# Ordering a mixture of experts by token count: blocks of two and of four experts, and the place of the overflow loop

## The chip, the cores and the metric

The kernel runs on one core of one Trainium2 chip. The metric is the device time of one execution in microseconds, 1274.82 us before the change (median of 3 runs, 1274.45 to 1277.62).

## The reference

An encoder trunk of two layers over 256 tokens of width 1024, in float32. Each layer is a mixer (layer 0: differential and latent attention; layer 1: dilated attention), a residual with layer norm, a hierarchical mixture of experts (MoE), and a second residual with layer norm. The MoE is what the change touches:

```
coarse = x @ w_group + b_group;  g = argmax(coarse)              # one of 4 groups
fine   = (x @ w_route + b_route)[group g]                        # 8 experts in it
top_v, top_i = top_k(fine, 2)                                    # 2 experts per token
gate   = softmax(coarse)[g] * softmax(top_v)
y     += gate * (silu(x @ w_gate[e]) * (x @ w_up[e])) @ w_down[e]   # for each chosen e
```

There are 32 experts; each has 1024 x 512 values in w_gate and in w_up and 512 x 1024 in w_down, 6 MiB in all. A layer has 512 assignments of a token to an expert, so an expert gets 16 on the average. Which expert gets how many is known only when the router has run.

## The kernel before, in words

**Stages.** The program is traced in one pass: mixer of layer 0, its MoE, mixer of layer 1, its MoE. Nearly all weights come through one ring of 16 tiles of 1 MiB (`RING`, `piece`, line 69), each filled by one DMA that SP issues. SP issues in order and waits until the tile's former content has been used. A planner orders the instructions of each engine when the program is built; `tc.issue_after` adds orders by hand.

**Routing** (`mixer_norm`, `halves`, `route`). TensorE makes the router's logits. On DVE, `route` finds for each token its group and its two experts, and with a matmul against a triangle the token's rank within each expert (`key`). `weights_of` makes the gates. `crowded` counts, for each expert, how many times 64 slots are overfull; the sum is the number of rounds of the overflow loop, `n_i`. All this stands at the start of a MoE, ahead of and beside the first gather.

**Pairs of experts.** The experts are taken in their own order, two at a time, 16 pairs a layer, with 64 token slots each (`CAP`). For every two pairs, `select` (L474) makes a one-hot matrix of 4 x 64 slots from `key`, and `gather` (L499) multiplies it with the normed tokens, in a high and a low half, to get the tokens' columns `xg`. `expert_pair` (L563, L583) then multiplies: g and u are 8 accumulating matmuls per expert, y is 8. The two experts of a pair write to partitions 0 to 63 and 64 to 127 of the same PSUM bank: the stationary operand has 64 columns, the moving one is the expert's own weights. `hidden` makes silu(g) * u and turns it; `slot_side` (L482 to L489) turns the one-hot matrix and picks each slot's gate; `combine` (L522 to L538) weights y, splits it in two halves and multiplies it back to the tokens, added to the residual `r` on DVE. In the last pair the residual is put into PSUM first (`carried`, L262, tile `fin`), and the combine adds to it there. `keep_clock` puts small matmuls where TensorE would pause.

**Weights of a pair.** `load_pair` issues 12 pieces a pair: gate, up, down; of each the first half of its columns for both experts, then the second. It is called one pair ahead. The mixers load the first pair's first pieces already (`EARLY`: 5 and 7).

**The overflow loop** (L681, L682) stands behind pair 11 (`LOOP_AFTER = 5` counts quads). All engines read `n_i` and run a loop of that many rounds; each round takes one expert with more than 64 tokens and does up to 64 of the rest. Ahead of the loop, 3 pieces of pair 12 have been issued (`AHEAD = 3`), the other 9 are issued behind it.

Of the kernel before, what the change touches and what calls it, by code (L numbers as in the profile page):

```python
# [25 lines left out]
MAX_EXTRA = (2 * T) // (CAP + 1)  # L26
# [8 lines left out]
LOOP_AFTER = 5  # L35
PIECE = 2048
AHEAD = 3
# [17 lines left out]
def trunk(ctx, tc, xT_d, x_d, wab_d, wla_d, wuq_d, wukv_d, woab_d, wc_d, wocd, wr_d, rb_d, gate_d, up_d, down_d,  # L55
# [325 lines left out]
    def route(pool, lg_ps, mvs, layer):  # L381
# [96 lines left out]
    def slot_side(pool, sel, ws, ne, name):  # L478
        n = ne * CAP
        b = bank("slot" + name)  # L480
        for c in range(2):
            nc.tensor.matmul(b[0:n, 0:ne], lhsT=sel[:, c].bitcast(F32), rhs=ws[:, c], start=c == 0, stop=c == 1)  # L482
        for c in range(2):
            nc.tensor.transpose(b[0:n, 128 * (c + 1):128 * (c + 2)], sel[:, c].bitcast(F32), ident)  # L484
        wcol = pool.tile([128, 1], F32, tag="wcol", name="wcol" + name)
        for s in range(ne):
            nc.vector.tensor_copy(wcol[CAP * s:CAP * s + CAP], b[CAP * s:CAP * s + CAP, s:s + 1])  # L487
# [66 lines left out]
    def expert_pair(pool, layer, p, ws, xg, side, r, fetch):  # L554
        name = f"_{layer}_{p}"
        o = 128 * (p % 2)
        gu = [bank("g" + name), bank("u" + name)]
        for j in range(2):
            for kk in range(KK):
                if p + j == 0 and kk == 4:  # L560
                    fetch(range(2, 4))
                for s in range(2):
                    up = nc.tensor.matmul(gu[j][64 * s:64 * s + 64], lhsT=xg[:, kk, o + 64 * s:o + 64 * s + 64],  # L563
                                     rhs=ws[j, s, kk // 4][:, kk % 4 * 512:kk % 4 * 512 + 512],
                                     start=kk == 0, stop=kk == KK - 1)
            if j == 0:
                accs = carried(r, name) if 2 * p + 2 == EXPERTS else None
# [7 lines left out]
        def o2(s):  # L575
            return slice(64 * s, 64 * s + 64)

        for k2 in range(2):
            for h in range(2):
                for k in (2 * k2, 2 * k2 + 1):  # L580
                    for s in range(2):
                        w0 = k % 2 * 1024 + h * 512
                        nc.tensor.matmul(y_ps[h][64 * s:64 * s + 64], lhsT=hT[:, k, o2(s)],  # L583
# [3 lines left out]
    def extra_block(pool, layer, parts, key, W, extra, r):  # L587
# [19 lines left out]
        v.tensor_scalar(dm[:, 1:2], dm[:, 1:2], -float(CAP), None, op0=OP.mult)  # L607
# [3 lines left out]
        sel = select(pool, col[:, 0], 1, name)  # L611
        side = slot_side(pool, sel, col[:, 1], 1, name)
# [25 lines left out]
    def moe(layer, acc, x_in, xn, after):  # L638
        with tc.tile_pool(name=f"moe{layer}", bufs=2) as pool:
# [6 lines left out]
            key, weights_of, crowded = route(pool, lg_ps, mvs, layer)  # L646
# [6 lines left out]
            load_pair(ws, layer, 0)  # L653
            W = None
            for q in range(EXPERTS // 4):
                name = f"_{layer}_q{q}"
                sel = select(pool, key[:, :, 4 * q:4 * q + 4], 4, name, 1 if q == 0 else 2)
# [6 lines left out]
                if q == 0:  # L664
                    with tc.issue_after(marks["sel"].ins):
                        W = weights_of()
                        extra, n_i = crowded()
                for p in (2 * q, 2 * q + 1):
                    if p + 1 < EXPERTS // 2:
                        load_pair(ws, layer, p + 1, AHEAD if p == 2 * LOOP_AFTER + 1 else 12)  # L670
                    o = 128 * (p % 2)

                    def side():
                        return slot_side(pool, sel[:, :, o:o + 128], W[:, :, 2 * p:2 * p + 2], 2, f"_{layer}_{p}")

                    last, accs = expert_pair(pool, layer, p, ws.pop(p), xg, side, r, fetch)
# [67 lines left out]
    def heads_ab(pool, xT):  # L744
# [222 lines left out]
        load_pair(moe_w[0], 0, 0, EARLY[0])  # L967
# [11 lines left out]
    def heads_c(pool, x, ws, res, gb):  # L979
# [87 lines left out]
        load_pair(moe_w[1], 1, 0, EARLY[1])  # L1067
# [164 lines left out]
```

## Time and profile before

| | us |
|---|---|
| runs of the kernel | 1274.45, 1274.82, 1277.62 |
| span of the profiled execution | 1273.0 |
| own time of the profiled execution around its span | not given; the median lies 1.8 above the span |
| busy: TensorE matmul / weight load | 1165.2 / 595.5 |
| busy: DVE / ACT / POOL | 459.3 / 260.9 / 109.6 |
| moved by DMA | 442.26 MB, mean 347 GB/s |

The span is cut into 40 slices of 31.8 us in the page's second part; a digit there is the busy share in tenths, and the line GB/s has what the DMA engines moved in each slice. Layer 0's MoE lies in slices 5 to 20, layer 1's in 25 to 40. Matmuls are pipelined, so the busy time of TensorE is not work at its peak.

### The profile page before, as it was taken

What the parts mean: (1) busy time and instruction counts of PE and PEld (TensorE: products, weight loads), DVE (VectorE), ACT (ScalarE), POOL (GpSimd) and SP (SyncE); (2) the same over time, 40 slices, a digit from 0 to 9 for tenths busy, and PEclk for the clock granted to TensorE, in tenths of its full rate; (3) what the DMA queues carried; (4) which work ended last, traced back from release to release, by engine and by line L of the source; (5) the groups of instructions that cost most, each with busy time, mean ns of one, the idle gap of its engine ahead of it and who ended that gap; (6) DMA issues with size and microseconds to landing.
All of it is one profiled execution on the core that took longest, in us unless ns stands there. A gap on an engine that the chain in (4) does not pass through costs nothing. (4 is left out here: it accounts for less than half of the span.)

```text
span 1273.0 us, 15010 instructions
## 1 busy us (share of the span) xinstructions
PE 1165.2 (92%) x5942; PEld 595.5 (47%) x5942; DVE 459.3 (36%) x949; ACT 260.9 (20%) x549; POOL 109.6 (9%) x89
## 2 busy tenths in 40 slices
PE   9998899999999998999798996999999999989996
PEld 7776334434343434343577774343434434343432
DVE  5787322212221222221777866222222212121213
ACT  5563111101110101011345542010111101010101
POOL 1014000000000000000623433000000000000001
PEclk9999899999999998999899998999999999999998
DMA  9737599999999966999944055999999999939993
GB/s 355 332 133 264 231 427 427 426 427 427 427 427 426 426 254 271 427 426 425 427 154 148 27 189 196 425 426 427 427 427 427 427 426 427 408 130 427 426 426 144
DMA packets 64009, 442.26 MB, mean 347 GB/s; under 512 B 7360, under 2 KB 8128, under 8 KB 11712
## 3 DMA queue, kind: packets, MB, share of 16 engines
q1 hardware_dynamic: 62496, 436.55, 82.8%
q0 software_dynamic: 1152, 4.19, 1.0%
q8 instruction: 48, 0.79, 0.2%
q10 hardware_dynamic: 288, 0.52, 0.1%
q14 instruction: 25, 0.20, 0.0%
HBM read 440.19 MB, written 1.05 MB: 347 GB/s over the span
## 5 line engine op out<-in xcount | busy, mean ns | idle before, releaser
L563 PE MATMUL u<-w,xg_q 128*64 128x512 f32 x1024 | 255.6, 595 | 0.0
L583 PE MATMUL y<-w,hT 128*64 128x512 f32 x1024 | 228.1, 596 | 24.3 <-DVE hT L514 24.3
L563 PE MATMUL g<-w,xg_q 128*64 128x512 f32 x1024 | 248.3, 600 | 0.0
L583 PEld LDWEIGHTS y<-w,hT 128*64 128x64 f32 x1024 | 84.1, 136 | 147.4 <-issue 115.8
L563 PEld LDWEIGHTS u<-w,xg_q 128*64 128x64 f32 x1024 | 78.6, 137 | 143.1 <-issue 141.1
L563 PEld LDWEIGHTS g<-w,xg_q 128*64 128x64 f32 x1024 | 73.9, 138 | 144.8 <-issue 126.3
L522 ACT ACTIVATE yh<-y,wcol 128x512 fp32r<-128x512 f32 x64 | 43.8, 688 | 422.8 <-PE y L583 422.8
L523 DVE SCALAR_TENSOR_TENSOR yl<-y,wcol,yh 128x512 fp32r<-128x512 f32 x64 | 47.8, 750 | 227.0 <-ACT yh L522 224.9
L508 DVE TENSOR_TENSOR h<-h,u 128x512 f32<-128x512 f32 x32 | 22.0, 688 | 235.7 <-PE u L563 235.7
L487 DVE COPY wcol<-slot 64x1 f32<-64x1 f32 x64 | 10.0, 156 | 220.7 <-PE slot L484 220.1
L243 POOL DMA_DIRECT2D gb<-in_lnrow_dram x8 | 4.7, 583 | 956.9 <-DVE h L508 473.5
L499 PE MATMUL xg_q<-sel_q,xh 128*128 128x256 f32 x256 | 69.3, 303 | 10.4 <-DVE sel_q L474 9.4
L538 DVE TENSOR_TENSOR r<-cb,r 128x512 f32<-128x512 f32 x112 | 71.1, 682 | 12.3 <-PE cb L529 12.3
L507 ACT ACTIVATE h<-g 128x512 f32<-128x512 f32 x32 | 19.1, 597 | 253.9 <-PE g L563 253.9
L499 PE MATMUL xg_q<-sel_q,xl 128*128 128x256 f32 x256 | 67.8, 299 | 0.0
L499 PEld LDWEIGHTS xg_q<-sel_q,xh 128*128 128x128 f32 x256 | 53.4, 209 | 14.7 <-DVE sel_q L474 8.4
L499 PEld LDWEIGHTS xg_q<-sel_q,xl 128*128 128x128 f32 x256 | 53.5, 209 | 0.6
L292 ACT ACTIVATE xg_q<-xg_q,pv 128x256 f32<-128x256 f32 x64 | 32.7, 561 | 90.6 <-PE xg_q L499 90.6
L529 PE MATMUL cb<-yl,selT 128*128 128x512 f32 x120 | 42.8, 430 | 1.2
L529 PE MATMUL cb<-yh,selT 128*128 128x512 f32 x120 | 41.8, 421 | 0.0
L513 PE MATMUL hT<-con,h 128*128 128x128 f32 x128 | 21.0, 286 | 20.8 <-DVE h L508 20.4
L294 DVE TENSOR_SCALAR xg_q<-xg_q,pv 128x256 f32<-128x256 f32 x64 | 31.7, 537 | 20.4 <-PE xg_q L499 20.4
(1043 smaller groups left out, 1419.4 us busy)
## 6 DMA issues: line engine op xcount, KB each, us to landing
w<-in_gate_dram SPq DMA_DIRECT2D x128, 1024.0 KB, 13.0
w<-in_up_dram SPq DMA_DIRECT2D x128, 1024.0 KB, 11.3
w<-in_down_dram SPq DMA_DIRECT2D x126, 1024.0 KB, 13.7
wqkc<-in_wc_dram SPq DMA_DIRECT2D x8, 1024.0 KB, 19.9
wqk<-in_wab_dram SPq DMA_DIRECT2D x4, 1024.0 KB, 13.8
wo<-in_woab_dram SPq DMA_DIRECT2D x4, 1024.0 KB, 10.9
gb<-in_lnrow_dram POOLq DMA_DIRECT2D x8, 512.0 KB, 6.6
wvc<-in_wc_dram SPq DMA_DIRECT2D x4, 1024.0 KB, 19.3
```

The source lines that it names most:

```text
L292: nc.scalar.activation(out, src, AF.Identity, bias=bb, scale=g)
L294: nc.vector.tensor_scalar(out, src, g, bb, op0=OP.mult, op1=OP.add)
L499: nc.tensor.matmul(b[:, k * n:(k + 1) * n], lhsT=parts[j][:, c, kk * 128:(kk + 1) * 128], rhs=sel[:, c], start=c + j == 0, stop=c + j == 2)
L507: marks["silu"] = nc.scalar.activation(h[0:n], g_ps[0:n], AF.Silu)
L508: nc.vector.tensor_tensor(h[0:n], h[0:n], u_ps[0:n], op=OP.mult)
L513: turn = nc.tensor.transpose(bv[:, k, 0:n], h[0:n, k * 128:(k + 1) * 128], ident[0:n, 0:n])
L522: last = nc.scalar.activation(yh[0:n, h], y_ps[h][0:n], AF.Copy, scale=wcol[0:n])
L523: nc.vector.scalar_tensor_tensor(yl[0:n, h], y_ps[h][0:n], wcol[0:n], yh[0:n, h].bitcast(F32), op0=OP.mult, op1=OP.subtract)
L529: last_mm = nc.tensor.matmul(b, lhsT=selT[0:n, c * 128:(c + 1) * 128], rhs=y[0:n, h], start=j == 0 and not accs, stop=j == 1)
L538: nc.vector.tensor_tensor(o, b, o, op=OP.add)
L563: up = nc.tensor.matmul(gu[j][64 * s:64 * s + 64], lhsT=xg[:, kk, o + 64 * s:o + 64 * s + 64], rhs=ws[j, s, kk // 4][:, kk % 4 * 512:kk % ...
L583: nc.tensor.matmul(y_ps[h][64 * s:64 * s + 64], lhsT=hT[:, k, o2(s)], rhs=ws[2, s, k // 2][:, w0:w0 + 512], start=k == 0, stop=k == 3)
```

## The change

The experts 0 to 3 stay as they are, in two pairs. The other 28 are ordered by how many tokens they have: DVE compares the counts of all with all (`ordered`, on tiles of 28 x 28 values), which gives each expert's place, the experts' numbers in that order (`ids`), and `key` and gates in that order (`keyS`, `WS`). The four fullest are taken in two pairs with 64 slots each, the other 24 four at a time with 32 slots each, on 32 partitions each: 10 blocks a layer instead of 16, with 5 gathers instead of 8. The weights of an ordered expert are fetched from an address that SP makes from its number: a register load (`value_load`) per expert. The count of overflow rounds uses 32 for the 24. The overflow loop stands behind block 8, ahead of the last block, of whose 24 pieces 16 are issued ahead of it.

```diff
@@ constants @@
-MAX_EXTRA = (2 * T) // (CAP + 1)
+SMALL = 32
+FIXED = 4
+HEAVY = 4
+SORTED = EXPERTS - FIXED
+BLOCKS = [(2, i) for i in range(0, FIXED + HEAVY, 2)]
+BLOCKS += [(4, i) for i in range(FIXED + HEAVY, EXPERTS, 4)]
+MAX_EXTRA = (2 * T) // (SMALL + 1)
-LOOP_AFTER = 5
+LOOP_AFTER = len(BLOCKS) - 2
-AHEAD = 3
+AHEAD = 16
@@ route @@
-        def crowded():
+        def ordered(W):
+            n, sh = SORTED, [128, SORTED, SORTED]
+            cnt = t([32], "cnt")
+            v.scalar_tensor_tensor(cnt, rk[0][:, 64:96], 32.0, desc32, op0=OP.mult, op1=OP.add)
+            at = cnt[:, FIXED:]
+            big = pool.tile([128, n, n], F32, tag="y0", name=f"big{layer}", bufs=1)
+            place = t([n], "place")
+            v.tensor_tensor(big, at[:, None, :].to_broadcast(sh), at[:, :, None].to_broadcast(sh), op=OP.is_ge)
+            v.tensor_reduce(place, big, axis=AX.X, op=OP.add)
+            one = pool.tile([128, n, n], F32, tag="y1", name=f"one{layer}", bufs=1)
+            v.tensor_tensor(one, place[:, None, :].to_broadcast(sh), iota[:, 0:n, None].to_broadcast(sh), op=OP.is_equal)
+            ids = t([n], "ids", I32)
+            f = t([n], "idf")
+            v.tensor_tensor(big, one, desc32[:, None, FIXED:].to_broadcast(sh), op=OP.mult)
+            v.tensor_reduce(f, big, axis=AX.X, op=OP.add)
+            v.tensor_scalar(ids, f, -1.0, float(EXPERTS), op0=OP.mult, op1=OP.add)
+            out = []
+            for src, name in ((key, "keyS"), (W, "WS")):
+                o = t([2, n], name)
+                for c in range(2):
+                    v.tensor_tensor(big, one, src[:, c, None, FIXED:].to_broadcast(sh), op=OP.mult)
+                    v.tensor_reduce(o[:, c], big, axis=AX.X, op=OP.add)
+                out.append(o)
+            lite = t([32], "lite")
+            v.memset(lite[:, 0:FIXED], 0.0)
+            v.tensor_scalar(lite[:, FIXED:], place, float(HEAVY), float(CAP - SMALL), op0=OP.is_gt, op1=OP.mult)
             extra = t([32], "extra")
-            v.tensor_scalar(extra, rk[0][:, 64:96], float(CAP), None, op0=OP.is_gt)
-            for j in range(2, T // CAP):
-                v.scalar_tensor_tensor(extra, rk[0][:, 64:96], float(CAP * j), extra, op0=OP.is_gt, op1=OP.add)
+            v.tensor_tensor(cnt, rk[0][:, 64:96], lite, op=OP.add)
+            v.tensor_scalar(extra, cnt, float(CAP), None, op0=OP.is_gt)
+            for j in range(2, T // CAP + 1):
+                v.scalar_tensor_tensor(extra, cnt, float(CAP * j), extra, op0=OP.is_gt, op1=OP.add)
             n_f = t([1], "n_f")
             v.tensor_reduce(n_f, extra, axis=AX.X, op=OP.add)
             n_i = t([1], "n_i", I32)
             v.tensor_copy(n_i, n_f)
-            return extra, n_i
-
-        return key, weights_of, crowded
-
-    def select(pool, keys, ne, name, step=2):
-        sel = pool.tile([128, 2, ne, CAP], F32R, tag="sel", name="sel" + name)
+            return ids, out, extra, lite, n_i
+
+        return key, weights_of, ordered
+
+    def select(pool, keys, ne, cap, name, step=2):
+        sel = pool.tile([128, 2, ne, cap], F32R, tag="sel", name="sel" + name)
         for c in range(0, 2, step):
-            sh = [128, step, ne, CAP]
-            marks["sel"] = nc.vector.tensor_tensor(sel[:, c:c + step], iota[:, None, None, :].to_broadcast(sh),
+            sh = [128, step, ne, cap]
+            marks["sel"] = nc.vector.tensor_tensor(sel[:, c:c + step], iota[:, None, None, 0:cap].to_broadcast(sh),
                                     keys[:, c:c + step, :, None].to_broadcast(sh), op=OP.is_equal)
         return sel.rearrange("p c e s -> p c (e s)")
 
...
@@ load and expert block @@
-    def load_pair(ws, layer, p, upto=12):
+    def load_block(ws, layer, p, upto=99, ids=None):
         w = ws.setdefault(p, {})
-        for i in range(len(w), upto):
-            j, o, e = i // 4, i // 2 % 2, i % 2
-            src = (gate_d, up_d, down_d)[j][layer, 2 * p + e, :, o * PIECE:(o + 1) * PIECE]
+        ne, first = BLOCKS[p]
+        which = ws.setdefault(("at", p), {})
+        for i in range(len(w), min(upto, 6 * ne)):
+            j, o, e = i // (2 * ne), i // ne % 2, i % ne
+            if e not in which:
+                at = first + e - FIXED
+                which[e] = first + e if at < 0 else nc.sync.value_load(ids[0:1, at:at + 1], min_val=0, max_val=EXPERTS - 1)
+            src = (gate_d, up_d, down_d)[j][layer]
+            at, cols = which[e], slice(o * PIECE, (o + 1) * PIECE)
+            src = src[at, :, cols] if isinstance(at, int) else src[bass.ds(at, 1), :, cols].rearrange("o p n -> (o p) n")
             name = f"w{j}_{layer}_{p}_{e}_{o}"
-            if (p, i) == (EXPERTS // 2 - 1, 11):
+            if (p, i) == (len(BLOCKS) - 1, 6 * ne - 1):
                 w[j, e, o] = piece_parts([(k * 1024, src[:, k * 1024:(k + 1) * 1024]) for k in range(2)], name)
             else:
                 w[j, e, o] = piece(src, name)
 
-    def expert_pair(pool, layer, p, ws, xg, side, r, fetch):
+    def expert_block(pool, layer, p, ws, xg, side, r, fetch):
         name = f"_{layer}_{p}"
+        ne = BLOCKS[p][0]
+        cap = 128 // ne
         o = 128 * (p % 2)
         gu = [bank("g" + name), bank("u" + name)]
         for j in range(2):
             for kk in range(KK):
                 if p + j == 0 and kk == 4:
                     fetch(range(2, 4))
-                for s in range(2):
-                    up = nc.tensor.matmul(gu[j][64 * s:64 * s + 64], lhsT=xg[:, kk, o + 64 * s:o + 64 * s + 64],
+                for s in range(ne):
+                    up = nc.tensor.matmul(gu[j][cap * s:cap * s + cap], lhsT=xg[:, kk, o + cap * s:o + cap * s + cap],
                                      rhs=ws[j, s, kk // 4][:, kk % 4 * 512:kk % 4 * 512 + 512],
                                      start=kk == 0, stop=kk == KK - 1)
...
@@ moe @@
-            load_pair(ws, layer, 0)
-            W = None
-            for q in range(EXPERTS // 4):
+            load_block(ws, layer, 0)
+            W = ids = None
+            for q in range(len(BLOCKS) // 2):
                 name = f"_{layer}_q{q}"
-                sel = select(pool, key[:, :, 4 * q:4 * q + 4], 4, name, 1 if q == 0 else 2)
+                ne, first = BLOCKS[2 * q]
+                cap = 128 // ne
+                if first < FIXED:
+                    keys = key[:, :, first:first + 2 * ne]
+                else:
+                    keys = keyS[:, :, first - FIXED:first - FIXED + 2 * ne]
+                sel = select(pool, keys, 2 * ne, cap, name, 1 if q == 0 else 2)
                 xg = keep.tile([128, KK, 4 * CAP], F32, tag=("x", "gb")[q % 2], name="xg" + name)
 
                 def fetch(k2s):
@@ -664,24 +710,26 @@
                 if q == 0:
                     with tc.issue_after(marks["sel"].ins):
                         W = weights_of()
-                        extra, n_i = crowded()
+                        ids, (keyS, WS), extra, lite, n_i = ordered(W)
                 for p in (2 * q, 2 * q + 1):
-                    if p + 1 < EXPERTS // 2:
-                        load_pair(ws, layer, p + 1, AHEAD if p == 2 * LOOP_AFTER + 1 else 12)
+                    if p + 1 < len(BLOCKS):
+                        load_block(ws, layer, p + 1, AHEAD if p == LOOP_AFTER else 99, ids)
                     o = 128 * (p % 2)
+                    at = BLOCKS[p][1]
 
                     def side():
-                        return slot_side(pool, sel[:, :, o:o + 128], W[:, :, 2 * p:2 * p + 2], 2, f"_{layer}_{p}")
-
-                    last, accs = expert_pair(pool, layer, p, ws.pop(p), xg, side, r, fetch)
+                        w = W[:, :, at:at + ne] if at < FIXED else WS[:, :, at - FIXED:at - FIXED + ne]
+                        return slot_side(pool, sel[:, :, o:o + 128], w, ne, cap, f"_{layer}_{p}")
+
+                    last, accs = expert_block(pool, layer, p, ws.pop(p), xg, side, r, fetch)
+                    if p == LOOP_AFTER:
+                        n = nc.values_load(n_i[0:1, 0:1], min_val=0, max_val=MAX_EXTRA)
+                        with tc.For_i(0, n):
+                            extra_block(pool, layer, parts, key, W, extra, lite, r)
+                        load_block(ws, layer, p + 1, 99, ids)
                 if q == 0:
                     with tc.issue_after(last_lg.ins):
                         keep_clock(clk, CLOCK)
-                if q == LOOP_AFTER:
-                    n = nc.values_load(n_i[0:1, 0:1], min_val=0, max_val=MAX_EXTRA)
-                    with tc.For_i(0, n):
-                        extra_block(pool, layer, parts, key, W, extra, r)
-                    load_pair(ws, layer, p + 1)
```

The parts left out pass the number of slots along (`slot_side`, `extra_block`) and rename.

## Rows read from the trace of the kernel before

**Rows 1.** The page, 40 slices of the span: GB/s in each.

```profile
GB/s 355 332 133 264 231 427 427 426 427 427 427 427 426 426 254 271 427 426 425 427 154 148 27 189 196 425 426 427 427 427 427 427 426 427 408 130 427 426 426 144
```

**Rows 2.** Window of 290 us: bounds, us, busy by engine, clock, DMA share, GB/s.

```profile
160.00:450.00 290.00, 274.45 (x1286) 115.03 (x1284) 68.63 (x124) 33.27 (x60) 0.00 (x0) 1.00 1.01 427
```

**Rows 3.** Waits, 150 to 464 us: engine and line, releaser, us, times, longest.

```profile
SPq L70 <- PE g L563: 99.3, 30, 9.0
...
PEld u L563 <- DMA w<-in_gate_dram: 0.3, 1, 0.3
```

**Rows 4.** Windows of 4 us around the loop, layer 0, then layer 1.

```profile
462.00:466.00 4.00, 4.00 (x22) 1.51 (x18) 0.00 (x0) 0.55 (x1) 0.00 (x0) 1.00 0.59 248
...
486.00:490.00 4.00, 1.26 (x6) 1.26 (x7) 1.86 (x3) 0.00 (x0) 0.00 (x0) 0.72 0.47 115
490.00:494.00 4.00, 4.00 (x20) 4.00 (x20) 0.99 (x2) 1.02 (x2) 0.00 (x0) 0.50 0.99 416
...
1108.00:1112.00 4.00, 4.00 (x22) 1.28 (x18) 0.00 (x0) 0.00 (x0) 0.00 (x0) 1.00 0.95 399
1112.00:1116.00 4.00, 4.00 (x24) 1.71 (x22) 0.31 (x2) 0.98 (x2) 0.00 (x0) 1.00 0.21 84
```

**Rows 5.** SP: timeline (start, us) in layer 0; waits at layer 1's loop.

```profile
451.36 36.21 SPq L70 DMA_DIRECT2D w<-in_gate_dram  x4
487.61 2.44 SPq L70 DMA_DIRECT2D w<-in_up_dram  x4
...
SPq L682 <- DVEq L681: 17.0, 1, 17.0
SPq L682 <- SPq L682: 11.8, 5, 2.5
```

**Rows 6.** Line L682 (the loop) on SP, layer 0: ns, first to last start.

```profile
L682 SPq EVENT_SEMAPHORE  x3: 17/17/17, 466.5 to 466.6; - x3
...
L682 SPq EVENT_SEMAPHORE  x9: 17/17/18035, 467.0 to 467.8; - x9
...
L682 SPq COMPARE_BRANCH  x1: 43/43/43, 486.8 to 486.8; - x1
```

**Rows 7.** Chain that ended last, layer 1's last pairs: start, us, what.

```profile
1141.53 7.02 PE g L563 x32
...
1229.36 1.72 PE fin L262 x4
...
1241.36 0.54 PE slot L482 x4
...
1242.17 7.01 PE u L563 x30
...
1251.91 7.11 PE y L583 x32
```

**Rows 8.** Timeline of TensorE at layer 0's end: start, us, line, operation.

```profile
605.71 7.14 PE L583 MATMUL y<-w,hT 128*64 128x512 f32 x32
...
615.75 3.52 PE L95 MATMUL clkn<-ones_b 128*128 128x128 bf16 x60
```

**Rows 9.** The page, costliest groups: one matmul of u.

```profile
L563 PE MATMUL u<-w,xg_q 128*64 128x512 f32 x1024 | 255.6, 595 | 0.0
```

**Rows 10.** Timeline of DVE, layer 0's MoE start; in brackets idle before.

```profile
135.09 0.68 DVE L474 TENSOR_TENSOR sel_q<-con,key 128x512 fp32r<-128x512 f32 x1
...
137.13 0.22 DVE L454 TENSOR_TENSOR oh<-oh 128x64 f32<-128x64 f32 x1
140.37 0.99 DVE L294 TENSOR_SCALAR xg_q<-xg_q,pv 128x256 f32<-128x256 f32 x2 [3.01 <-PE xg_q L499]
151.88 0.69 DVE L508 TENSOR_TENSOR h<-h,u 128x512 f32<-128x512 f32 x1 [10.52 <-PE u L563]
```

**Rows 11.** Lines L681 (register load) and L70 (weight pieces): ns; landing in us.

```profile
L681 SPq TENSOR_LOAD <-n_i x2: 283/375/467, 455.3 to 1102.3; - x2
...
DMA to landing us min/median/max: 5.0/12.8/22.1
```

More of the change, by code (lines that the diff above doesn't have):

```diff
@@ L465, in crowded, with slot_side @@
             v.tensor_copy(n_i, n_f)
-            return extra, n_i
-        return key, weights_of, crowded
-    def select(pool, keys, ne, name, step=2):
-        sel = pool.tile([128, 2, ne, CAP], F32R, tag="sel", name="sel" + name)
+            return ids, out, extra, lite, n_i
+        return key, weights_of, ordered
+    def select(pool, keys, ne, cap, name, step=2):
+        sel = pool.tile([128, 2, ne, cap], F32R, tag="sel", name="sel" + name)
         for c in range(0, 2, step):
-            sh = [128, step, ne, CAP]
-            marks["sel"] = nc.vector.tensor_tensor(sel[:, c:c + step], iota[:, None, None, :].to_broadcast(sh),
+            sh = [128, step, ne, cap]
+            marks["sel"] = nc.vector.tensor_tensor(sel[:, c:c + step], iota[:, None, None, 0:cap].to_broadcast(sh),
                                     keys[:, c:c + step, :, None].to_broadcast(sh), op=OP.is_equal)
         return sel.rearrange("p c e s -> p c (e s)")
-    def slot_side(pool, sel, ws, ne, name):
-        n = ne * CAP
+    def slot_side(pool, sel, ws, ne, cap, name):
+        n = ne * cap
         b = bank("slot" + name)
@@ L486, in slot_side @@
         for s in range(ne):
-            nc.vector.tensor_copy(wcol[CAP * s:CAP * s + CAP], b[CAP * s:CAP * s + CAP, s:s + 1])
+            nc.vector.tensor_copy(wcol[cap * s:cap * s + cap], b[cap * s:cap * s + cap, s:s + 1])
         selT = pool.tile([128, 256], F32R, tag="selT", name="selT" + name)
@@ L566, in expert_pair @@
             if j == 0:
-                accs = carried(r, name) if 2 * p + 2 == EXPERTS else None
+                accs = carried(r, name) if p + 1 == len(BLOCKS) else None
         side = side()
@@ L573, in expert_pair @@
         y_ps = [bank("y0" + name), bank("y1" + name)]
-        def o2(s):
-            return slice(64 * s, 64 * s + 64)
         for k2 in range(2):
@@ L580, in expert_pair, with extra_block @@
                 for k in (2 * k2, 2 * k2 + 1):
-                    for s in range(2):
+                    for s in range(ne):
                         w0 = k % 2 * 1024 + h * 512
-                        nc.tensor.matmul(y_ps[h][64 * s:64 * s + 64], lhsT=hT[:, k, o2(s)],
+                        nc.tensor.matmul(y_ps[h][cap * s:cap * s + cap], lhsT=hT[:, k, cap * s:cap * s + cap],
                                          rhs=ws[2, s, k // 2][:, w0:w0 + 512], start=k == 0, stop=k == 3)
         return combine(pool, y_ps, side, 128, r, name, p == 0, accs), accs
-    def extra_block(pool, layer, parts, key, W, extra, r):
+    def extra_block(pool, layer, parts, key, W, extra, lite, r):
         name = f"_x{layer}"
@@ L606, in extra_block @@
         v.tensor_reduce(dm[:, 1:2], rem, axis=AX.X, op=OP.add)
-        v.tensor_scalar(dm[:, 1:2], dm[:, 1:2], -float(CAP), None, op0=OP.mult)
+        v.tensor_tensor(rem, lite, oh, op=OP.mult)
+        v.tensor_reduce(dm[:, 0:1], rem, axis=AX.X, op=OP.add)
+        v.scalar_tensor_tensor(dm[:, 1:2], dm[:, 1:2], -float(CAP), dm[:, 0:1], op0=OP.mult, op1=OP.add)
         v.tensor_scalar(col[:, 0], col[:, 0], dm[:, 1:2], None, op0=OP.add)
@@ L610, in extra_block @@
         e = nc.sync.value_load(eid[0:1, 0:1], min_val=0, max_val=EXPERTS - 1)
-        sel = select(pool, col[:, 0], 1, name)
-        side = slot_side(pool, sel, col[:, 1], 1, name)
+        sel = select(pool, col[:, 0], 1, CAP, name)
+        side = slot_side(pool, sel, col[:, 1], 1, CAP, name)
         xg = pool.tile([128, KK, CAP], F32, tag="x_xg", name="x_xg", bufs=1)
@@ L645, in moe @@
             parts = (xh, xl)
-            key, weights_of, crowded = route(pool, lg_ps, mvs, layer)
+            key, weights_of, ordered = route(pool, lg_ps, mvs, layer)
             low = halves(xn, mvs, xh, xl)
@@ L966, in heads_ab @@
         jobs.next()
-        load_pair(moe_w[0], 0, 0, EARLY[0])
+        load_block(moe_w[0], 0, 0, EARLY[0])
         ws = op.prep_piece(3)
@@ L1066, in heads_c @@
         attend(6)
-        load_pair(moe_w[1], 1, 0, EARLY[1])
+        load_block(moe_w[1], 1, 0, EARLY[1])
         ws = op.prep_piece(3)
```

## The prediction

> **What bounds the kernel now.** I read the table of 40 slices first. The line of GB/s [rows 1] shows two plateaus of 425 to 427, one per MoE stage, each with a hole near its last third (254 and 271 in layer 0, 130 in layer 1). A long window inside the first plateau has 427 GB/s at a granted clock of 1.00 [rows 2], so one piece of 1 MiB (1.0486 MB) takes 2.456 us, a pair of experts (12 pieces) 29.5 us.
>
> The waits of the same stretch [rows 3] then say which of the two, transfers or TensorE, ends last: SP waits for slots of the ring that matmuls still hold (99.3 us on g alone), while the weight loads of TensorE waited 0.3 us for a transfer. So TensorE is busy without a gap for data, and the transfers run at their plateau all the same: the two are equally fast, a pair costs some 29.5 us on either, and a change that helps one alone shows little while the other is at its limit.
>
> The hole is the overflow loop. In layer 0 the transfers fall from 426 GB/s to nothing and come back near 488 us [rows 4]. Why, SP's own queue shows [rows 5]: after three pieces of pair 12 it stops at the loop (L682). In layer 1 it waited there for itself five times, at most 2.5 us each, the length of one piece: it waits for each outstanding transfer to land. Then it waits 17 us for DVE. In layer 0 that first wait ended at 466.5 us [rows 6], 2.2 us after the last byte at 464.3 (248 of 426 GB/s in the window from 462), and all engines left the loop at 486.8. Nobody passes before what was prefetched has landed and every engine has arrived. TensorE meanwhile went on with pair 11 and lost only the loop itself (1.26 us busy of 4 in the window from 486) and some clock behind it (0.50 in the next): of a hole of 24 us in the transfers it paid a few.
>
> The ends that I count from: the last y of layer 1 ends at 1251.91 + 7.11 = 1259.02 [rows 7], that of layer 0 at 605.71 + 7.14 = 612.85 [rows 8]. What follows these ends I leave alone.
>
> **The change, part by part.**
>
> *Four experts at once.* A matmul instruction of g, u or y takes 595 ns [rows 9], but 32 of them take 7.02 us [rows 7], 0.219 each: the two column groups run beside each other. With four groups of 32 columns the count per expert is the same. From below: 0.110 each if four groups run beside each other as two do; from above 0.219, if nothing more overlaps than now. I take 0.110, since the streaming part of one instruction (0.43 us for two now) is what the groups share, and the 60 small matmuls with their weight loads in 3.52 us [rows 8] show that 0.059 us for a load and a matmul can be issued. A block of four then needs 3 x 7.0 us and about 10 us around it (in [rows 7] a pair's 29.5 less its g, u and y leaves 8), some 31 us; even at 0.219 it needs 52. Its 24 pieces need 59.0 us. So from block 4 on the transfers are the bound, not TensorE; the 16 slots suffice, since four pieces land in 9.8 us, are used up 3.5 us later, and their slots are wanted 16 x 2.456 = 39 us after the landing.
>
> The Trainium skill, TensorE: Matmul & The Clock Gate, section Part 3 (packing small matmuls), gives 2.38 times for three column tiles of 32 at 512 columns, that is 79% of full overlap. By it an instruction would take about 0.136 us (an estimate), g, u and y 1.7 us more each, and the sum below would be about 1246. The trace shows 97% for two groups; no run here shows four.
>
> *Stream up to the loop.* The first four pairs are as before, so the transfers are too, until the 147th piece of a layer (12 pairs and 3), which landed at 464.3 in layer 0 and at 1112.5 in layer 1 (399 and 84 GB/s in its last two windows [rows 4]). There the old stream stopped; the new one goes on. The new loop stands behind block 8 (168 pieces), with 16 of the last block's 24 sent ahead: piece 184. That is 37 pieces, 90.9 us later: 555.2 and 1203.4.
>
> *The loop at its new place.* Moved past it on SP are the 16 DMAs; behind SP's wait stand the last 8 pieces, and behind the loop on TensorE the whole last block. The same wait [rows 5, 6] now covers 39 us of prefetch. TensorE, done with block 8 long before, idles for it. From the last byte to the exit: 2.2 us to see it, 1.3 for the semaphores up to 467.8, 0.9 for the exit: TensorE starts the last block at S = 559.6 and 1207.8. (Block 9 needs no gather; block 8 brought it.)
>
> *The last block.* From S on TensorE: g 7.0 us; the clock falls in such a pause (0.50, so 1.2 GHz, in the window from 490 after the old loop [rows 4]), and I let half of g's work run so, which adds 3.3; fin 3.4 (eight, four in 1.72), slot 0.8, u 7.0; 2.7 from u's end to y; y 7.1 [rows 7]. Sum 31.3. The transfers beside it: the first slot is free when g's fourth row of blocks is through, S + 6.5 with the slow clock; the first bytes 1.7 us after SP's issue (about 487.2, the end of its long row [rows 5]; 115 GB/s in the window from 486, so 1.1 us at full rate, from 488.9 [rows 4]); 8 pieces 19.6; the landing seen 2 later; two and a half for what of y waits for the last piece: S + 32.3. The two end together; I take 32.3. So y ends at 591.9 and 1240.1: gains of 20.9 and 18.9 us.
>
> *The sort on DVE.* 13 operations over 784 elements and about as many small ones come in behind the first sel. 64 elements take 0.22, 512 take 0.68 [rows 10]; by their slope 784 take 0.96: 12.5 us, with the small ones 14.5 a layer. DVE is otherwise idle 3.0 us before the second affine at 140.37 and 10.5 us before h [rows 10], and until then the ring is full and nothing is transferred, so what delays TensorE's first g is lost outright. Bounds: 0 (all in the gaps) and 14.5 (all ahead of the first affine). The router's own small operations and the next sel (0.68) lie in the same gaps there without holding the affine up; I take 1 us a layer, the overhang of one operation. If the cover of h fails, yh is next.
>
> *Register loads on SP.* 28 a layer, 0.28 to 0.47 us each by the like load for the loop [rows 11]. The numbers exist some 5 of the large operations behind the weights (137.13 [rows 10]), near 145, and block 2's first piece waits for a slot that y of block 0 frees, after 153. Pieces take 12.8 us (median) from issue to landing [rows 11], which hides the four loads ahead of a block: cost 0; the other end, with the queue dry each time, is 1.9 us for each of 16 blocks, 30 in all. A DMA with its address in a register is not in the trace; from below it costs what a plain one does, from above 2.46 us, where SP would become the bound.
>
> *Fewer gathers, slots, combines.* 10 blocks for 16, 5 gathers for 8: nothing, since TensorE is not the bound there any more.
>
> *Overflow.* By the reference's routing of its default inputs the eight fullest of experts 4 to 31 have 37, 36, 35, 29, 29, 25, 25, 22 tokens in layer 0 and 30, 25, 25, 23, 21, 21, 20, 19 in layer 1, experts 0 to 3 at most 22: the loop runs no round, before or after.
>
> **The sum.** 20.9 + 18.9 - 2 x 1 = 37.8 us off. The profiled span is 1273.0; the page gives nothing of the time around it, and the median of the runs is 1274.82, 1.8 above the span, which I keep. 1273.0 - 37.8 + 1.8 = 1237.0.
>
> **Rivals.**
>
> *The loop is hidden.* If the loop does not hold TensorE until the 16 pieces are in, nothing stalls: piece 192 lands 45 pieces (110.5 us) after the 147th, 574.8 and 1223.0, y ends about 6.7 later (receipt 2.2, rest of y at the slow clock 4.5): gains 31.3 and 29.3, less 2: 1216. Sixteen pieces ahead speak for it; SP's five waits of one piece [rows 5] against.
> The Trainium skill, DMA: Bandwidth & Descriptors, section Rules for kernel authors, says to issue a DMA early and wait for it late so that it overlaps with compute; by that the sum would be this rival's 1216. Here the wait is not the consumer's but the loop's, which the rule does not speak of.
>
> *Slower: four groups are no faster than two.* Place: the last block, where behind the loop nothing hides TensorE. At 0.219 us g, u and y cost 6.9 more each, 20.6 a layer, which takes back 41 of the 40 won; with the sort and a longer cold g about 1279. It decides from 0.21 us an instruction; beyond 0.255 every block of four also outlasts its transfers. For it: four different moving operands at once occur nowhere in the trace. Against: two run at 97%.
>
> *Slower: SP becomes the bound* where a piece with a register address takes over 2.57 us to issue (37.8 / 336 such pieces above 2.456). Plain ones are issued every 0.6 us behind the old loop (4 in 2.44 [rows 5]).
>
> *The sort goes first.* DVE does it ahead of the first affine in both layers: 2 x 13.5 more, 1264.
>
> **How the numbers follow.** Forecast as worked out, own range 1226 to 1250: 0.60. Hidden loop: 0.12. Sort first, or groups that overlap by half (1250 to 1270): 0.15. Groups no faster: 0.06. SP: 0.03. The rest, 0.04, lies around no change. Faster than by 0.3% (what a measurement of this kernel can tell, its runs lying within 0.25%): 0.60 + 0.12 + 0.15 and a little of the rest, 0.88; same 0.03; slower 0.09. The range 1214 to 1262 takes in the hidden loop and most of the late sort.
>
> **What would show it.** Right: GB/s at 427 without a hole until about 555 us, then a hole of some 12 us, not 24; TensorE idle some 30 us or more at a clock of 0.50 ahead of the last block; 64 instructions of g in about 7 us (at full clock); y of layer 0 ending near 592; TensorE waiting for weights throughout the small blocks. Wrong: no hole, g of a block of four in 14 us, DVE's 784-element rows ahead of the first affine, or SP's register loads with an idle transfer queue behind them.

## The result and the profile after

The changed kernel takes 1242.05 us (median of 4 runs, 1241.71 to 1242.86); the kernel before, beside it on the same chip, took 1274.63. Ratio 0.974, interval 0.9726 to 0.9755: faster by 32.6 us, where 37.8 were forecast. The profiled execution of after took 1242.86 us with a span of 1240.6.

Transfers, the page of after (GB/s in 40 slices, now of 31.0 us), the answer to [rows 1]:

```profile
GB/s 348 357 136 234 177 427 426 426 427 426 427 426 428 426 425 427 427 427 279 426 230 126 33 204 153 402 426 426 426 426 427 427 427 426 426 426 427 427 277 216
```

One hole a layer is left, one slice from the end of the plateau (279 and 277), where before had two slices a layer (254 and 271, then 408 and 130). Windows of 4 us at layer 0's loop in after, with the columns of [rows 4]:

```profile
556.00:560.00 4.00, 0.00 (x0) 0.00 (x0) 0.00 (x0) 0.00 (x0) 0.00 (x0) 0.50 0.98 414
560.00:564.00 4.00, 0.00 (x0) 0.00 (x0) 0.00 (x0) 0.00 (x0) 0.00 (x0) 0.50 0.32 133
564.00:568.00 4.00, 3.55 (x20) 0.92 (x24) 0.00 (x0) 0.00 (x0) 0.00 (x0) 0.50 0.01 4
568.00:572.00 4.00, 4.00 (x44) 1.06 (x40) 0.00 (x0) 0.00 (x0) 0.00 (x0) 0.96 0.28 47
572.00:576.00 4.00, 4.00 (x22) 1.45 (x15) 0.00 (x0) 1.88 (x2) 0.00 (x0) 1.00 0.96 395
```

Against 427 these windows miss some 10.7 us of transfer (10.9 in layer 1; before missed 24.7 and 23.5). TensorE stands idle ahead of it; its timeline in after, layer 0's last block (start, us; in brackets the idle time before), answers to [rows 7, 8]:

```profile
564.45 8.97 PE L604 MATMUL g<-w,xg_q 128*32 128x512 f32 x64 [34.09 <-SPq L727]
573.35 3.70 PE L268 MATMUL fin<-r,con 128*128 128x512 f32 x8
576.98 7.07 PE L604 MATMUL u<-w,xg_q 128*32 128x512 f32 x64
...
588.19 7.69 PE L621 MATMUL y<-w,hT 128*32 128x512 f32 x64
```

64 instructions of u take 7.07 us where 32 took 7.02: four column groups cost nothing more than two. In the small blocks TensorE waits for data, which it did not before (0.3 us in [rows 3]). Waits of TensorE's weight loads in after, 160 to 500 us (us, times, longest):

```profile
PEld u L604 <- DMA w<-in_up_dram: 36.5, 22, 2.8
PEld g L604 <- DMA w<-in_gate_dram: 34.1, 18, 2.3
PEld y L621 <- DMA w<-in_down_dram: 28.4, 24, 2.2
```

So TensorE now waits for the transfers, and what either kernel pays at the loop follows from that.

### The profile page after: what moved, and what is told of

It reads as the page before. It is cut to its first block, busy times and chain, and to the rows that moved or that the text cites. A ratio compares the mean times of both kernels' runs of the same rounds, so it can differ in the third digit from the quotient of the medians.

```text
span 1240.6 us, 14798 instructions
## 1 busy us (share of the span) xinstructions
PE 984.8 (79%) x5534; PEld 472.0 (38%) x5534; DVE 401.7 (32%) x861; ACT 220.2 (18%) x477; POOL 109.5 (9%) x89
## 5 line engine op out<-in xcount | busy, mean ns | idle before, releaser
L604 PE MATMUL g<-w,xg_q 128*32 128x512 f32 (+1 forms) x1024 | 193.7, 647 | 105.8 <-SPq L727 69.0
L621 PE MATMUL y<-w,hT 128*32 128x512 f32 (+1 forms) x1024 | 221.0, 601 | 39.1 <-DMA w<-in_down_dram 23.9
L604 PE MATMUL u<-w,xg_q 128*32 128x512 f32 (+1 forms) x1024 | 206.2, 652 | 46.6 <-DMA w<-in_up_dram 46.6
L604 PEld LDWEIGHTS g<-w,xg_q 128*32 128x32 f32 (+1 forms) x1024 | 51.3, 124 | 228.7 <-issue 146.0
L621 PEld LDWEIGHTS y<-w,hT 128*32 128x32 f32 (+1 forms) x1024 | 58.7, 116 | 188.0 <-issue 100.8
L604 PEld LDWEIGHTS u<-w,xg_q 128*32 128x32 f32 (+1 forms) x1024 | 52.8, 125 | 177.7 <-issue 91.8
L531 PE MATMUL xg_q<-sel_q,xh 128*128 128x256 f32 x160 | 41.9, 296 | 1.9 <-DVE cs L440 1.0
L570 DVE TENSOR_TENSOR r<-cb,r 128x512 f32<-128x512 f32 x64 | 40.3, 681 | 4.2 <-PE cb L561 4.2
L531 PE MATMUL xg_q<-sel_q,xl 128*128 128x256 f32 x160 | 41.0, 292 | 0.0
L312 POOL TENSOR_TENSOR r<-r,gb 128x1024 f32<-128x1024 f32 x12 | 30.1, 2538 | 0.0
## 6 DMA issues: line engine op xcount, KB each, us to landing
w<-in_gate_dram SPq DMA_DIRECT2D x128, 1024.0 KB, 19.5
w<-in_up_dram SPq DMA_DIRECT2D x128, 1024.0 KB, 19.5
wqk<-in_wab_dram SPq DMA_DIRECT2D x4, 1024.0 KB, 14.4
wo<-in_woab_dram SPq DMA_DIRECT2D x4, 1024.0 KB, 10.9
```

The lines of the kernel that those rows point to most:

```text
L312: nc.gpsimd.tensor_tensor(x[:, c], x[:, c], gb[:, j], op=op)
L531: nc.tensor.matmul(b[:, k * n:(k + 1) * n], lhsT=parts[j][:, c, kk * 128:(kk + 1) * 128], rhs=sel[:, c], start=c + j == 0, stop=c + j == 2)
L570: nc.vector.tensor_tensor(o, b, o, op=OP.add)
L604: up = nc.tensor.matmul(gu[j][cap * s:cap * s + cap], lhsT=xg[:, kk, o + cap * s:o + cap * s + cap], rhs=ws[j, s, kk // 4][:, kk % 4 * 512 ...
L621: nc.tensor.matmul(y_ps[h][cap * s:cap * s + cap], lhsT=hT[:, k, cap * s:cap * s + cap], rhs=ws[2, s, k // 2][:, w0:w0 + 512], start=k == ...
```

## Experiments

All are compared with the kernel before on their own chip (1274.9 to 1275.7), so ratios compare better than times.

**The loop taken out of the kernel after.**

```diff
-n = nc.values_load(n_i[0:1, 0:1], ...)
-with tc.For_i(0, n):
-    extra_block(pool, layer, parts, key, W, extra, lite, r)
```

> The changed kernel without its overflow loop; it leaves out the overflow rounds, of which these inputs need none. Theory (the loop lets nobody pass before the 16 prefetched pieces have landed, and the ring is full then, so the transfers stop for 10.7 and 10.9 us a layer): the transfers run at 427 GB/s to the end of both layers, TensorE is not idle for 34 us ahead of the last block, y ends some 4 to 6 us behind the last piece: 9 to 10.5 us less per layer, 1221 to 1224. Rival (the last block is bound by TensorE, not by the transfers): TensorE starts it some 30 us earlier, so y would end as soon as its data is in and the gain is the same, but the hole in the transfers would stay. Rival (the hole is covered elsewhere): 1242, no gain.

1221.12 (1219.89 to 1222.37), ratio 0.9577 [0.9561, 0.9593], as expected. The loop costs after 21 us, as much as its two holes (10.7 and 10.9). GB/s has no hole in either layer (slices of 30.5 us):

```profile
GB/s 346 372 139 229 178 426 427 426 427 426 427 426 427 426 425 428 426 427 426 425 211 127 36 206 140 390 427 427 426 427 427 427 427 427 427 425 427 427 427 203
```

**The loop taken out of the kernel before.** The same lines.

> The kernel before without its overflow loop; it leaves out the overflow rounds, of which these inputs need none. Theory (TensorE set the pace before, and of the 24 us hole in the transfers it paid only its own idle time of 4.3 us and about 2 us of slow clock per layer): 1260 to 1264, transfers with some waits for slots or level with TensorE. Rival (the transfers set the pace before, so the hole was paid in full): 1226.

1267.64 (1262.06 to 1268.92), 0.9924 [0.9898, 0.9951]: 8 us, where 11 to 15 were expected. The two holes of some 24 us at the old loop cost little, since in before TensorE ends last: without the loop layer 1's transfers end near 1224, y at 1253.0. A window of 4 us, then TensorE's timeline, without the loop:

```profile
1224.00:1228.00 4.00, 4.00 (x16) 1.24 (x15) 0.52 (x1) 0.00 (x0) 0.00 (x0) 1.00 0.01 4
...
1245.91 7.14 PE L583 MATMUL y<-w,hT 128*64 128x512 f32 x32
```

TensorE is 29 us behind the transfers, three quarters of what the ring holds (16 x 2.456 = 39 us). Without their loops the two kernels lie 46.5 us apart: this is what the change is worth without the loop.

**Eight pieces ahead of the loop for 16.**

```diff
-AHEAD = 16
+AHEAD = 8
```

> The changed kernel with 8 instead of 16 pieces ahead of the loop. Theory (the hole is what lies between the last landing and the next issue: 2.2 us to see it, 2.2 for the loop, 1.7 to the first byte, and on top of it, with 16 ahead, the first half of g, because the ring is full): with 8 slots free the first half of g falls out, the hole shrinks from 10.7 to about 6 us, TensorE idles about 15 us at the loop instead of 34: 4 to 5 us less per layer, 1232 to 1234. Rival (pieces ahead are what hides the loop, fewer hide less): the hole grows by up to 13 us a layer towards the old one, up to 1268.

1230.31 (1229.0 to 1231.65), 0.9643 [0.9627, 0.9659], a little better than expected. The hole shrinks to 5.8 us (6.3 in layer 1); windows of 4 us:

```profile
540.00:544.00 4.00, 0.14 (x4) 0.14 (x8) 0.00 (x0) 0.00 (x0) 0.00 (x0) 0.50 0.32 135
544.00:548.00 4.00, 4.00 (x20) 0.86 (x22) 0.00 (x0) 0.00 (x0) 0.00 (x0) 0.51 0.44 115
548.00:552.00 4.00, 4.00 (x44) 1.20 (x40) 0.00 (x0) 0.00 (x0) 0.00 (x0) 1.00 1.01 422
```

TensorE's idle time falls from 34.09 to 14.38 us, and SP shows why the hole is shorter. Timeline of TensorE, then of SP, with eight ahead:

```profile
543.86 9.05 PE L604 MATMUL g<-w,xg_q 128*32 128x512 f32 x64 [14.38 <-SPq L727]
...
545.11 4.39 SPq L76 DMA_DIRECT2D w<-in_up_dram  x8
```

And SP of after:

```profile
570.01 4.82 SPq L76 DMA_DIRECT2D w<-in_down_dram  x7
```

With eight slots free SP issues 1.25 us after TensorE has started again; with 16 unused pieces in 16 slots it waits 5.6 us, until g has used up the first.

**No sort.** The order of the experts is fixed and no register is loaded.

```diff
-                        ids, (keyS, WS), extra, lite, n_i = ordered(W)
+                        extra, lite, n_i = plain()
+                        keyS, WS = key[:, :, FIXED:], W[:, :, FIXED:]
...
-                which[e] = first + e if at < 0 else nc.sync.value_load(ids[0:1, at:at + 1], min_val=0, max_val=EXPERTS - 1)
+                which[e] = first + e
```

> The changed kernel with its blocks of two and four, but the experts in their own order: no sort on DVE, no register loads on SP, fixed addresses; it leaves out the tokens beyond 32 of an expert in a block of four. Theory (the sort costs 1.1 us in layer 0 and 1.3 in layer 1, where the transfers come back later at the start of the MoE; register loads and addresses cost nothing): 1239 to 1240.5. Rival (the register loads or the addresses cost transfer time as well): below 1237. Rival (the sort is free): 1242.

1233.18 (1231.07 to 1233.35), 0.9664 [0.9647, 0.968]: missed, and no clean test. The planner put layer 1's loop after 364 weight DMAs, where after has 377: 3 pieces ahead for 16, so its hole there was 5.9 us, and most of the gain is the loop's (2.5 us more lie in mixer 1, which had no dip of the clock, see below). Layer 0, with 16 ahead, is the clean half: it lost the same 1.1 us at the start of its MoE without the sort, and from its first g to its last y it took 459.3 us, with the sort 458.9.

**The place alone.** Kernel before with the loop ahead of the last pair.

```diff
-LOOP_AFTER = 5
-AHEAD = 3
+LOOP_AFTER = EXPERTS // 2 - 2
+AHEAD = 12
...
```

`LOOP_AFTER` counts pairs here; the lines of the loop, left out, move with it.

> The kernel before, with its pairs, but its overflow loop moved ahead of the last pair, with all 12 pieces of that pair ahead of it: the move alone. Theory (nobody passes the loop before the prefetch has landed, and with pairs TensorE sets the pace): TensorE waits at the loop for 12 pieces (29.5 us) and then has the whole last pair, some 31 us, before it with nothing beside it; against the kernel before without a loop (1268) that is some 20 to 24 us more per layer: 1305 to 1318, slower than before. Rival (the new place and the longer prefetch hide the loop): 1262 to 1268.

1266.45 (1264.06 to 1270.5), 0.993 [0.9908, 0.9953]. My theory fell, the rival held. TensorE's timeline of this kernel at layer 0's loop:

```profile
579.14 7.09 PE L563 MATMUL g<-w,xg_q 128*64 128x512 f32 x32 [2.24 <-SPq L679]
```

2.24 us idle: TensorE is so far behind the transfers that what was prefetched lands while it still works on the pair before. That is layer 0 alone: in layer 1 the planner put the loop after 376 of 386 weight DMAs, 3 pieces of the last pair ahead for 12. The hole there is 25 us, and TensorE idles 2.0 us all the same. With pairs this kernel gains some 9 us, as much as taking the loop out does (8).

**The blocks of four alone.** The kernel after with the loop one block earlier, at about its old piece (147 of 192).

```diff
-LOOP_AFTER = len(BLOCKS) - 2
-AHEAD = 16
+LOOP_AFTER = len(BLOCKS) - 3
+AHEAD = 3
```

> The changed kernel with its loop at the old place, behind 24 experts (block 7), with 3 pieces ahead: the blocks of four without the move. Theory (what the loop costs is the hole that its wait leaves in the transfers, and not its place): the 3 pieces land some 7 us behind block 7's last, the engines arrive some 12 us behind it, the transfers come back some 4 us later, a hole of 8 to 10 us: within 4 us of the changed kernel, 1237 to 1242. Rival (the new place is what won): 1255 or more.

1231.45 (1229.21 to 1232.69), 0.9661 [0.9644, 0.9677], better than expected: the hole is 6.9 and 6.8 us where 8 to 10 were put. So fours alone give 43 us, the place alone 9, both together 32.6. The 10 us that the move with its 16 pieces costs in the kernel with fours are not the place's, since the new place with 8 ahead takes 1230.31.

**Sort, register loads and register addresses with pairs.** 14 ordered pairs of 64, loop at the old place.

```diff
-SMALL = 32
-BLOCKS += [(4, i) for i in range(FIXED + HEAVY, EXPERTS, 4)]
+SMALL = 64
+BLOCKS += [(2, i) for i in range(FIXED + HEAVY, EXPERTS, 2)]
...
-LOOP_AFTER = len(BLOCKS) - 2
+LOOP_AFTER = 11
...
-AHEAD = 16
+AHEAD = 3
```

> The changed kernel with 14 ordered pairs of 64 slots in place of the blocks of four, and the loop at its old place (pair 11, 3 pieces ahead): the kernel before with the sort, the register loads and the addresses in registers. Theory (the sort is hidden, register loads and addresses cost nothing): 1273 to 1277. Rival (they cost what the first layer's start lost, 1.1 us or more a layer): 1277 to 1279. Rival (SP's issue becomes the bound): 1285 or more.

1271.9 (1269.68 to 1273.07, 9 runs), 0.9972 [0.9959, 0.9984]: 3 us faster than before and 1 us below the range of the theory, for a reason that no trace here shows. All this machinery costs nothing that can be measured where TensorE sets the pace.

**Twelve pieces ahead.** `AHEAD = 12` in the kernel after.

> The changed kernel with 12 pieces ahead of the loop. Theory (above 12 the ring is full at the loop and the first half of g lies in the hole; at 12 and below it doesn't): the hole is 5.5 to 6.5 us as with 8 ahead, TensorE idles some 25 us, 1229 to 1233. Rival (the hole grows with the number of pieces ahead): 8 to 8.5 us, 1235 to 1238.

1231.28 (1228.7 to 1232.99), 0.9649 [0.9627, 0.9671], as expected, with holes of 6.5 and 5.8 us. TensorE idles 24.6 us ahead of the loop here, 14.4 with eight ahead, at the same total: the idle time alone is not the price.

**The layer norm's rows loaded late.** POOL's timelines show a transfer that the prediction had not counted. Before, then after:

```profile
603.95 1.11 POOL L243 DMA_DIRECT2D gb<-in_lnrow_dram  x2 [473.53 <-DVE h L508]
```

```profile
447.60 1.12 POOL L249 DMA_DIRECT2D gb<-in_lnrow_dram  x2 [315.12 <-PE u L604]
```

These two 512 KB loads of the second layer norm's rows share a tile's tag with every second gather. The last of 8 gathers had that tag; of 5 it has the other, so the tile is free two blocks earlier and the loads run ahead of the last weights. Held back:

```diff
+        if behind is not None:
+            nc.gpsimd.tensor_scalar(gb[:, 0:2, 0:192], behind, 0.0, None, op0=OP.mult)
         for j in range(2):
             nc.gpsimd.dma_start(gb[:, j], ...)
...
```

`behind` is h of the last block; the lines that pass it are left out.

> The kernel after, with one difference: the two 512 KB loads of the second layer norm's rows (gb, 1.05 MB a layer) start when the last block's h is ready, behind all expert weights; a small GpSimd operation holds them. In the kernel after they were issued at 447.6 us, in the middle of the weight stream, because a gather's tile with the same tag is free two blocks earlier with five gathers than with eight; before the change they were issued at 604.0, behind the weights. Theory: transfers are the bound, so these 2.46 us a layer (1.05 MB at 427 GB/s) are on the path ahead of the loop. Expected 1237.1 (1242.05 less 4.9), last byte ahead of the loop 2.5 us earlier in layer 0, y of layer 0 near 593.4. Rival one, that the loads cost nothing where they are since the loop's hole is set otherwise: 1242. Rival two, that they land too late for the layer norm then: 1244 or more.

1237.25 (1235.88 to 1238.87), 0.97 [0.9682, 0.9717]. The total is as expected, but the way is not: u of layer 0 ended 2.6 us earlier, y did not. TensorE's timeline:

```profile
585.62 5.37 PE L624 MATMUL y<-w,hT 128*32 128x512 f32 x44
591.64 1.91 PE L624 MATMUL y<-w,hT 128*32 128x512 f32 x12 [0.65 <-DMA w<-in_down_dram]
593.99 1.90 PE L624 MATMUL y<-w,hT 128*32 128x512 f32 x8 [0.44 <-DMA w<-in_down_dram]
```

The late loads ran beside the last pieces, and y waited for these. Of the profile's gain 2.7 us lie in mixer 1, whose clock did not dip (below), 1.0 in layer 1's MoE.

**The same with eight pieces ahead, and with the loop at the old place.**

> The same late loads of the layer norm's rows, with 8 pieces of the last block issued ahead of the loop instead of 16. Theory: the two gains add up, 1230.3 less 4.9, 1225.4. Rival, that with 8 ahead TensorE and no longer the transfers sets the end of the last block: 1228 to 1230.

> The same late loads, with the loop one block earlier (behind block 7, 3 pieces of block 8 ahead). Theory: 1231.45 less 4.9, 1226.5, the same as with 8 ahead at the new place within 1.5 us, since a loop costs some 9 to 10 us at either place once the ring holds few unused pieces. Rival, that the old place gains more because the last block's receipt is no longer behind the loop: below 1224.

1229.93 (1228.52 to 1231.46), 0.9648 [0.9631, 0.9665], and 1229.81 (1228.72 to 1231.63), 0.9647 [0.963, 0.9663]: no gain over 8 ahead (0.9643) and none beyond the intervals over the old place (0.9661). Both theories (1225.4 and 1226.5) fell. The first one's rival has the number, but not the reason: TensorE does not set the end, it waits for data. Its waits for the last block's pieces of w_down in layer 0, with 8 ahead, then with late rows as well (us, times, longest):

```profile
PE y L621 <- DMA w<-in_down_dram: 1.1, 2, 0.6
```

```profile
PE y L624 <- DMA w<-in_down_dram: 3.7, 2, 2.1
```

Loads that are held only until h is ready still compete with the last pieces.

**No such loads.**

```diff
-            nc.gpsimd.dma_start(gb[:, j], ...)
+            if which % 2:
+                nc.gpsimd.memset(gb[:, j], 1.0 - j)
+            else:
+                nc.gpsimd.dma_start(gb[:, j], ...)
```

An odd `which` is the second layer norm of a layer.

> The kernel after (16 pieces ahead of the loop) without the loads of the second layer norm's rows in both layers; GpSimd fills the tile with ones and zeros, so this part of the layer norm is left out. With those loads held back to the last block's h, u of layer 0 ended 2.4 us earlier, but y did not (596.1 for 595.9): the loads then ran beside the last expert pieces, y waited twice for them, and most of the gain in the profile came from mixer 1, whose granted clock had no dip there. Theory: transfers set the end of each MoE, so 1.05 MB less, wherever it stood, gives 2.46 us a layer at y's end: y of layer 0 at 593.4 plus or minus the start's 0.5, total 1237.1 with the dip in mixer 1's clock, 1234.7 without it. Rival: TensorE's own 31 us behind the loop set the end, then y's end stays within 0.5 us of 595.9 and the total at 1242 or, without the dip, 1239.6.

1234.84 (1234.24 to 1235.68), 0.9686 [0.967, 0.9702]. Layer 0's last y in its trace:

```profile
583.06 7.53 PE L624 MATMUL y<-w,hT 128*32 128x512 f32 x64
```

It ends at 590.6 for 595.9, earlier than the theory's 593.4, and the total is 2.3 us below the theory's 1237.1 with the dip. 1.9 of the 5.3 us are an earlier start of the MoE, so 3.4 us are gained in it, and 2.3 in layer 1 (its first g to its last y: 456.7 for 459.0). The 2.46 us of transfer are on the path, within a microsecond; the rival, by which y's end would stay, fell.

## Why the prediction held, and where its sum was off

**Four experts at once** was right, and fully: 0.110 us an instruction. The estimate from the 2.38 times for three column tiles, which the Trainium skill, TensorE: Matmul & The Clock Gate, gives in section Part 3 (packing small matmuls), was 0.136; this trace disagrees with it for four tiles of these shapes (7.07 us for 64, 8.7 by the estimate). That the transfers become the bound followed, as the waits show; the rivals "four groups no faster" and "SP the bound" fell.

**The loop at its new place** was right in kind: each outstanding transfer has to land before anyone passes. SP's waits in after, 500 to 566 us, the answer to [rows 5]:

```profile
SPq L727 <- SPq L727: 18.6, 6, 6.4
```

That contradicts the rival "hidden loop", 1216, and the 1221 without the loop show what it would have been worth. The rule of the Trainium skill that went with it (DMA: Bandwidth & Descriptors, section Rules for kernel authors: issue the DMA early, wait late) can be kept in its first half only, since the loop itself waits: 16 pieces early take 1242, eight 1230. The "2.2 us to see it" were read from windows of 4 us as if the last bytes had come at the full rate; windows of 1 us from 462 in before have 418, 303, 188 and 82 GB/s, so the last bytes came near 466 and were seen at 466.5. The sum is not touched, since it counts from that landing.

**The hole** was forecast at some 12 us (4.4 to TensorE's start, 6.5 of g, 1.7 to the first byte) and measured 10.7 and 10.9; of g it took 5.6 in layer 0. From S to the end of y, put at 32.3, it took 31.4 and 31.0.

**The stream up to the loop** holds the step that failed: "The first four pairs are as before, so the transfers are too, until the 147th piece". SP's issue of that piece and its landing before, then of the 147th and the 184th after:

```profile
L70 SPq DMA_DIRECT2D w<-in_gate_dram x1: 328/328/328, 454.8 to 454.8; - x1
...
DMA to landing us min/median/max: 11.7/11.7/11.7
```

```profile
L76 SPq DMA_DIRECT2D w<-in_gate_dram x1: 338/338/338, 450.7 to 450.7; - x1
...
DMA to landing us min/median/max: 22.0/22.0/22.0
...
L76 SPq DMA_DIRECT2D w<-in_up_dram x1: 333/333/333, 544.1 to 544.1; - x1
...
DMA to landing us min/median/max: 19.5/19.5/19.5
```

The 147th piece was seen to land at 466.5 before and at 472.7 after, 6.3 us later. "37 pieces, 90.9 us later" held: the 184th came at 563.6. What the step left out are the two loads of layer norm rows, 2.46 us more a layer, which landed at 456.3 and 460.3, ahead of the 147th piece. Without them, in the twelfth experiment, that piece landed at 467.9, 4.9 us earlier, of which 1.9 are the start's. The rest of the 6.3 us is the later start of the MoE (2.1, below) and 1.7 more, of which the sum had put down 1 for the sort.

**The sort** was put at 1 us a layer. Its large operations took the 0.96 of the slope, and the gathers' affines came between them. Timeline of DVE in after, the answer to [rows 10]:

```profile
134.81 0.97 DVE L470 TENSOR_TENSOR big<-cnt 128x784 f32<-128x784 f32 x1
135.84 0.99 DVE L300 TENSOR_SCALAR xg_q<-xg_q,pv 128x256 f32<-128x256 f32 x2
...
143.29 0.53 DVE L300 TENSOR_SCALAR xg_q<-xg_q,pv 128x256 f32<-128x256 f32 x1
143.75 0.96 DVE L483 TENSOR_TENSOR big<-one,key 128x784 f32<-128x784 f32 x1
```

The transfers do lose 1.1 us at this place in layer 0, but the kernel without the sort lost as much there, so the cause of this 1 us stays open; it isn't shown to be the sort. That the size came out right is luck.

**Register loads at nothing** held: 56 of them at 0.27 us (median) on SP, and the transfers stay at 427 GB/s; the seventh experiment bounds it for pairs.

**"What follows these ends I leave alone"** was not safe. From the end of layer 0's y to layer 1's first g before takes 170.0 us, after 171.7. The granted clock dips in mixer 1 of after at a place where it stays at 1.00 before (third column from the end); windows of after, then of before, at the same work:

```profile
668.00:672.00 4.00, 2.93 (x11) 2.28 (x12) 3.45 (x7) 1.26 (x3) 1.20 (x2) 0.84 0.27 49
672.00:676.00 4.00, 4.00 (x15) 3.20 (x14) 1.04 (x2) 1.31 (x3) 0.00 (x0) 0.73 0.54 213
```

```profile
684.00:688.00 4.00, 2.59 (x11) 2.09 (x12) 3.87 (x9) 1.66 (x4) 1.66 (x2) 1.00 0.21 33
688.00:692.00 4.00, 4.00 (x18) 3.10 (x18) 2.07 (x3) 1.68 (x3) 0.00 (x0) 1.00 0.62 233
```

Variants of after with the dip (without the loop; eight ahead; without the rows) take 171.2 to 171.6 for this stretch, those without it (twelve ahead; old place; no sort; all three with late rows) 168.8 to 169.3: among them the dip goes with some 2.4 us. It isn't the change's own: the kernel before without its loop has the dip too and takes 172.0. With the loop moved alone the clock falls there to 0.57 in one window, and the stretch takes 169.9, no longer than before. So a price of the dip is not shown, and what sets it off stays open.

**The sum** in the profiled executions: last y of layer 1 at 1259.0 before and 1226.6 after, 32.4 earlier for 37.8. Layer 0's y came 17.0 earlier for 19.9. Of that gap 2.1 are a later start that shows within the first 25 us of the program and differs between executions (the other variants have it 0.5 to 2.0 smaller, twelve ahead 1.2 larger), 2.5 the rows and 0.7 not resolved, less 2.3 from the 184th piece's landing to y's end. Mixer 1 adds 1.7. Layer 1's MoE adds 0.8 (17.1 for 17.9): rows 2.5 and 0.7 not resolved, less 2.4 from the landing on. So terms of some 10 us were missing, and the last blocks gave 4.7 of them back: that the sum came within 5 us is in part luck. The time around the span, kept at 1.8, was 2.3 in after.

**What beats both.** Five variants lie at 1229.8 to 1231.5 and can't be told apart: 8 or 12 ahead, the old place, and late rows with 8 ahead or the old place. The simplest is the kernel after with `AHEAD = 8`, 12 us below it.

## What to carry to other kernels

Before moving a barrier, ask which engine is behind. While TensorE lagged the transfers by 29 us, a loop that all engines enter cost 8 us a run for 48 us of holes; once TensorE had caught up, it cost 21 us for 21.6 us of holes, all of them. Ahead of such a loop, prefetch less than the ring holds, so that the DMA queue finds free slots at the exit: with 8 or 12 of 16 slots used, two loops cost some 9 to 10 us. When the number of uses of a rotating tile changes, see which other loads share its tag: their start moves too, and where transfers are the bound their bytes go to the front of the queue.

## What the runs showed of the hardware

Four fp32 matmuls with 32 stationary columns each and four different moving operands run beside each other as well as two with 64 do (0.110 us each for 0.219). With mostly 8 pieces outstanding, as in the plateaus of after, a piece takes 19.5 us (median) from issue to landing; with 4 to 7, as in before, it took 12.8, at the same 427 GB/s. A DMA with its address in a register moves at the same 427 GB/s as a plain one. 1 MB on another queue takes its share from the weight stream: while the late rows came in (584 to 596 us), all queues together moved 376 to 428 GB/s, no more than the weights alone, and y waited for its weights.
